# A hybrid decoder layer on one core: the first group of seven products in each feed-forward gets its weight sums and its accumulating transfer earlier

## The chip, the cores and the metric

The kernel runs on one core of one Trainium2 chip, as one program of one launch. The metric is the device time of an execution in microseconds (us). A profiled execution gives a trace of every instruction beside it.

## The reference, cut to what matters

One layer over 256 tokens and a model width of 1024, all in float32: a half-step feed-forward, a mixer (two kinds of attention, gated and merged), a second half-step feed-forward and a last norm.

```python
def swiglu(x, w_gate, w_up, w_down):
    return (jax.nn.silu(x @ w_gate) * (x @ w_up)) @ w_down
...
        h = h + FFN_RES * swiglu(rms_norm(h, ffn1_norm[l]), ffn1_w_gate[l], ffn1_w_up[l], ffn1_w_down[l])
        h = h + hybrid_mixer(rms_norm(h, mix_norm[l]), positions, w_in[l], b_gate[l],
                             w_branch_moba[l], w_branch_sb[l], w_out[l])
        h = h + FFN_RES * swiglu(rms_norm(h, ffn2_norm[l]), ffn2_w_gate[l], ffn2_w_up[l], ffn2_w_down[l])
    return rms_norm(h, final_norm)
```

The gate and up weights are 1024 x 2816, the down weights 2816 x 1024.

## The kernel before, in words

**Weights.** All weights stand in one stream of 376 tiles of 128 x 512, loaded two at a time: a chunk `raw{c}` holds tiles 2c and 2c+1 and is one transfer of 512 KB, issued by SP (`load`, line 188). Six chunks are in SBUF at a time (`RAW = 6`): the load of a chunk waits until the engines have read the chunk whose buffer it takes. A weight is used in two parts so that float32 precision is kept: ScalarE writes the rounded part `wh`, VectorE the rest `wl = raw - wh` (lines 228 and 229, or 232 and 233 with a gain), and TensorE makes three products from them (lines 370 to 372). The step that makes one pair `wh`, `wl` is `split`, and there is one for each *item*. Items are numbered in the order of use. Twelve pairs have buffers.

**Order of the work.** Nothing is scheduled by cost around the change: in both feed-forwards each engine executes its instructions in the order in which the program issues them (`manual_schedule`). Each `unit` issues three matmuls, lets one tick pass for the tasks that run beside (`weave`), and calls `W.pump()`, which issues at most one more `split`, if it is no more than `ahead` items ahead of the item in use. `ahead` is 7 for most of a feed-forward and 11 from its last gate-and-up block on.

**A feed-forward.** Eleven blocks of 8 items make the gate and up products, 256 hidden columns each (`gu_f`); the two halves of the tokens, t = 0 and 1, take turns with t = 1 two items behind. A block's result stands in a PSUM bank of a ring of three. `hidden` empties it: ScalarE's Silu (line 558), VectorE's product (line 559) into `sh_f`, VectorE's transpose in squares (line 567) into `hs_f`. For each pair of blocks, 16 small transfers `hm_f<-hs_f` of 32 KB (line 531) put the squares where the down product wants them, a few ticks apart, among the weight loads on SP's queue for the first four pairs of blocks and on GpSimd's for the last two. ScalarE and VectorE then split that too (`hth_f`, `htl_f`). The bank of block 9, t = 0 is taken again by block 10, t = 1.

**Sevens.** The down product works on groups of 2 x 128 hidden rows. Five of a feed-forward's groups use seven products in place of eight (a Strassen-like scheme), group 0 among them, which comes straight behind the gate and up blocks. Seven items j = 0 to 6 belong to such a group, with four tiles s to s+3 of the stream. Four of the seven weights are sums of tiles:

- tile s+1 gets tile s added by an accumulating transfer from HBM, issued by GpSimd (`summed`, line 200), nine items ahead of the group (`AHEAD_ADD = 9`);
- VectorE makes T2 = tile(s+1) + tile(s+3), T3 = T2 - tile(s), T4 = T2 + tile(s+2) (line 208), each in the `split` of the items j = 1, 2 and 3, just ahead of that item's `wh`. Items 4, 5 and 6 use T3, T2 and T4.

In the first feed-forward, items 80 to 87 are the last gate-and-up block, and items 88 to 94 are the seven of group 0, with chunks 44 and 45. The second feed-forward has the same order 259 items later, with chunks 166 and 167. The rows of its trace stand some 356.9 us behind the first one's.

Of the kernel before, what the change touches and what calls it, by code (L numbers as in the profile page):

```python
# [21 lines left out]
KD = D // P  # L22
FB = FF // 256
# [5 lines left out]
CH = 2  # L29
# [5 lines left out]
W_FFN2 = W_OUT + 2 * KD  # L35
# [30 lines left out]
AHEAD = 7  # L66
AHEAD_DOWN = 11
AHEAD_ADD = 9


INV_FREQ = [
# [30 lines left out]
class Weave:  # L102


    def __init__(self):
        self.now = 0
        self.tasks = []

    def add(self, gen, delay=0, long=False):
        self.tasks.append([self.now + delay, gen, long])  # L110
# [28 lines left out]
def _items():  # L139

    out, n = [], 0

    def plain(count):
        nonlocal n
        out.extend((n + i, None) for i in range(count))
        n += count

    for f in range(2):
        plain(FB * KD)
        for g in range(KF // 2):  # L150
            if g in SEVENS[f]:
                out.extend((n, j) for j in range(7))
                n += 4
            else:
                plain(4)
        if f == 0:
            plain(W_FFN2 - W_IN)
    assert n == N_TILES
    return out


class Weights:


    def __init__(self, nc, pool, early, sums, stream, gain, bufs, ahead):
        self.early, self.sums, self.items = early, sums, _items()
        self.nc, self.pool, self.stream, self.gain = nc, pool, stream, gain
        self.bufs, self.ahead = bufs, ahead
        self.loaded = self.ready = self.freed = self.at = 0
        self.raw, self.parts, self.behind = {}, {}, {}  # L170
        self.made, self.ahead_of = {}, {}
        self.depth = RAW
        for i, (s, j) in enumerate(self.items):
            if j == 0:
                self.ahead_of[i - AHEAD_ADD] = s

    def load(self, n, tiles=0):

# [18 lines left out]
    def summed(self, s):  # L197

        self.load(s // CH + 1)
        self.nc.gpsimd.dma_start(self.tile(s + 1), self.source(s), accum_op=ALU.add)  # L200

    def seventh(self, s, j):

        if 0 < j < 4:
            op, b, o = ((self.nc.vector.tensor_add, 3, "T2"), (self.nc.vector.tensor_sub, 0, "T3"),
                        (self.nc.vector.tensor_add, 2, "T4"))[j - 1]
            self.made[s, o] = self.sums(f"{o}_{s}")
            op(self.made[s, o], self.made[s, "T2"] if j > 1 else self.tile(s + 1), self.tile(s + b))
        raw = self.made.pop((s, f"T{(3, 2, 4)[j - 4]}")) if j > 3 else self.tile(s + (0, 2, 3, 1)[j])
        return raw, (s // CH, s // CH + 1) if j == 3 else ()  # L210

    def split(self):
        i = self.ready
        if i in self.ahead_of:
            self.summed(self.ahead_of.pop(i))
        s, j = self.items[i]
        used = (s // CH,) if s % CH == CH - 1 else ()
        if j is None:
            self.load(s // CH + 1)
            raw = self.tile(s)  # L220
        else:
            self.load(s // CH + (2 if j else 1))
            raw, used = self.seventh(s, j)
        hi = self.pool.tile([P, 512], F32R, name=f"wh{i}", tag="wh", bufs=self.bufs)
        lo = self.pool.tile([P, 512], F32R, name=f"wl{i}", tag="wl", bufs=self.bufs)
        g = self.gain(i)
        if g is None:
            self.nc.scalar.copy(hi, raw)  # L228
            self.nc.vector.tensor_sub(lo, raw, hi.bitcast(F32))  # L229
        else:  # L230
            for s in HALVES if i == 0 else (slice(0, 512),):
                self.nc.scalar.activation(hi[:, s], raw[:, s], AF.Copy, scale=g)  # L232
                self.nc.vector.scalar_tensor_tensor(lo[:, s], raw[:, s], g, hi[:, s].bitcast(F32),  # L233
                                                    op0=ALU.mult, op1=ALU.subtract)
        self.parts[i] = hi, lo
        self.ready += 1
        if i in self.behind:
            self.behind.pop(i)()
        for c in used:
            del self.raw[c]  # L240
            self.load(c + 1 + self.depth)
# [19 lines left out]
def hybrid_layer_kernel(ctx, tc, x, xt, pos, g_final, bgate, wstream, out):  # L261
# [164 lines left out]
    class Normed:  # L426
# [6 lines left out]
        def half(self, c, src=None):  # L433
            s = slice(c * 512, c * 512 + 512)
            src = h[self.t][:, s] if src is None else src
            tp = two_banks(f"tp_{self.nm}{self.t}{c}")[:, 0:512]
            for k in range(4):
                nc.tensor.transpose(tp[:, k * P:(k + 1) * P], src[:, k * P:(k + 1) * P], ident)
            split(self.parts[0][:, s], self.parts[1][:, s], tp)
            self.there.add(c)  # L440

        def moved(self, c):

            s = slice(c * 512, c * 512 + 512)
            if self.nm == "u" and self.t == 0:
                W.depth = RAW - 2
            q = big(f"{self.nm}q{self.t}{c}", F32)
            nc.vector.transpose(slots(q[:, 0:512], 4), plain(h[self.t][:, s]))
            W.ahead = AHEAD
            yield D_SQUARES  # L450
            queues = [nc.sync, nc.gpsimd]
            if self.nm == "u":
                queues = [nc.gpsimd, nc.sync, nc.gpsimd] if self.t else [nc.gpsimd, nc.scalar]
            elif self.t == 0:
                queues = [nc.gpsimd] + queues * 2
            yield from exchange(q[:, 512:1024], q[:, 0:512], 4, queues, 1)
            yield D_EIGHT
            split(plain(self.parts[0][:, s]), plain(self.parts[1][:, s]), slots(q[:, 512:1024], 4))
            self.there.add(c)

        @staticmethod
        def moved_both(c, norms):

            s = slice(c * 512, c * 512 + 512)
            squares, moved = [big(f"{norms[0].nm}{i}{c}", F32) for i in "sm"]
            for t in range(2):
                nc.vector.transpose(slots(squares, 8)[:, t:t + 7:2], plain(h[t][:, s]))
                yield None if t == 0 else D_SQUARES
            yield from exchange(moved, squares, 8, [nc.sync, nc.gpsimd], 1)
            yield D_BOTH  # L470
            for t in range(2):
                split(plain(norms[t].parts[0][:, s]), plain(norms[t].parts[1][:, s]), slots(moved, 8)[:, t:t + 7:2])
                norms[t].there.add(c)
                yield 1
# [815 lines left out]
```

## Time and profile before

| | |
|---|---|
| median of 3 runs | 546.92 us (546.83 to 547.07) |
| the profiled execution's own time | 547.5 us |
| its span, first to last instruction | 545.8 us |
| TensorE (PE) busy | 538.0 us, 99% of the span |
| VectorE (DVE) busy | 453.5 us, 83% |
| ScalarE (ACT) busy | 355.5 us, 65% |
| GpSimd (POOL) busy | 122.1 us, 22% |
| DMA, mean | 210 GB/s |

A row of a timeline has the start and the duration in us, the engine ("q" stands for its queue of DMA issues), the line of the kernel, what is written and read, the shapes and how many instructions the row merges; in brackets stands the idle time ahead of it with what ended it. Of a DMA, the row shows the issue; when it lands is read from the view of DMA issues, in us from the start of the issue. Buffer numbers are left out of the trace's names: `raw`, `wl` and `T` stand for all chunks, rests and sums.

### The profile page before, as it was taken

The page shows a single profiled execution, that of the slowest core. Times are in us where ns is not written, and L with a number is a line of the kernel's source. Part 1 is how long each engine was busy: PE and PEld are TensorE (multiplying, and loading weights), DVE is VectorE, ACT ScalarE, POOL GpSimd, SP SyncE. Part 2 cuts the span into 40 slices and gives each one's busy share as a digit, 9 for nine tenths or more (in the row PEclk, how much of TensorE's full clock was granted, in tenths as well). Part 3 has the DMA queues.
Part 4 walks back from the last instruction along what each step waited for, and adds up shares of the span by engine and source line. Part 5 has one row for each costly group of instructions (what it writes and reads, how often), then busy time and mean ns, then how long its engine had stood idle before and what let it go on. Part 6 is the DMA issues. An engine that isn't in the chain of part 4 may idle for free.

```text
span 545.8 us, 8032 instructions
## 1 busy us (share of the span) xinstructions
PE 538.0 (99%) x2460; PEld 444.4 (81%) x2460; DVE 453.5 (83%) x817; ACT 355.5 (65%) x620; POOL 122.1 (22%) x235
## 2 busy tenths in 40 slices
PE   9999999999999999999999999999999999999995
PEld 6888888888888888888888888888888888888884
DVE  5797799889999767889888888877667887899995
ACT  6776566667683777677875775466566566666843
POOL 2400000025503575022022200383000000265100
PEclk9999999999999999999999999999999999999998
DMA  8976765787866786455555354677657767787712
GB/s 280 406 263 220 239 209 184 231 254 225 257 225 191 274 261 217 154 155 191 170 161 175 125 188 153 195 244 233 215 180 223 221 201 236 233 227 237 238 49 77
DMA packets 44058, 114.84 MB, mean 210 GB/s; under 512 B 8512, under 2 KB 16240, under 8 KB 44016
## 3 DMA queue, kind: packets, MB, share of 16 engines
q1 hardware_dynamic: 37440, 106.68, 59.1%
q0 software_dynamic: 5904, 7.17, 6.0%
q10 hardware_dynamic: 672, 0.49, 0.3%
q8 instruction: 19, 0.31, 0.3%
q14 instruction: 23, 0.19, 0.1%
HBM read 104.87 MB, written 1.05 MB: 194 GB/s over the span
## 4 chain that ended last, share of the span: by engine, by line
PE 97%; DMA 1%; ACT 0%; SPq 0%; DVE 0%; issue 0%; ACTq 0%
PE gu_f L371 13%; PE gu_f L372 13%; PE gu_f L370 13%; PE in L370 7%; PE in L372 7%; PE in L371 7%; PE dn_f L371 5%; PE dn_f L372 5%; PE dn_f L370 5%; PE wo L372 1%; PE wo L370 1%; PE wo L371 1%; PE gu_f L383 1%; PE gu_f L384 1%; PE gu_f L386 1%; DMA raw<-in_wstream 1%
## 5 line engine op out<-in xcount | busy, mean ns | idle before, releaser
L233 DVE SCALAR_TENSOR_TENSOR wl<-raw,first,wh 128x512 fp32r<-128x512 f32 (+1 forms) x257 | 180.1, 742 | 24.0 <-ACT wh L232 23.5
L232 ACT ACTIVATE wh<-raw,first 128x512 fp32r<-128x512 f32 (+1 forms) x257 | 168.6, 714 | 26.1 <-PE gu_f L372 7.5
L229 DVE TENSOR_TENSOR wl<-raw,wh 128x512 fp32r<-128x512 f32 x120 | 78.7, 681 | 2.4 <-ACT wh L228 2.4
L228 ACT CAST wh<-raw 128x512 fp32r<-128x512 f32 x120 | 68.1, 618 | 18.2 <-PE bb L372 5.5
L371 PE MATMUL gu_f<-wl,zh 128*128 128x512 f32 x176 | 68.5, 389 | 0.0
L370 PE MATMUL gu_f<-wh,zh 128*128 128x512 f32 x176 | 68.5, 389 | 0.0
L372 PE MATMUL gu_f<-wh,zl 128*128 128x512 f32 x176 | 68.5, 389 | 0.0
L370 PE MATMUL in<-wh,uh 128*128 128x512 f32 x160 | 63.6, 397 | 0.0
L372 PE MATMUL in<-wh,ul 128*128 128x512 f32 x160 | 62.5, 391 | 0.0
L371 PE MATMUL in<-wl,uh 128*128 128x512 f32 x160 | 62.4, 390 | 0.0
L372 PE MATMUL gu_f<-wh,xl 128*128 128x512 f32 x144 | 56.0, 389 | 0.0
L370 PE MATMUL gu_f<-wh,xh 128*128 128x512 f32 x144 | 56.0, 389 | 0.0
L371 PE MATMUL gu_f<-wl,xh 128*128 128x512 f32 x144 | 56.0, 389 | 0.0
L200 POOL DMA_DIRECT2D raw<-in_wstream x10 | 9.4, 938 | 190.3 <-DVE cs_f L585 89.5
L370 PE MATMUL dn_f<-wh,hth_f 128*128 128x512 f32 x112 | 43.7, 390 | 0.0
L372 PE MATMUL dn_f<-wh,htl_f 128*128 128x512 f32 x112 | 43.6, 389 | 0.0
L371 PE MATMUL dn_f<-wl,hth_f 128*128 128x512 f32 x112 | 43.6, 389 | 0.0
L531 POOL DMA_DIRECT2D hm_f<-hs_f x64 | 34.3, 681 | 22.7 <-DMA raw<-in_wstream 9.3
L370 PEld LDWEIGHTS gu_f<-wh,zh 128*128 128x128 f32 x176 | 33.0, 188 | 6.9
L372 PEld LDWEIGHTS gu_f<-wh,zl 128*128 128x128 f32 x176 | 33.0, 188 | 6.8
L371 PEld LDWEIGHTS gu_f<-wl,zh 128*128 128x128 f32 x176 | 33.0, 188 | 6.8
L372 PEld LDWEIGHTS in<-wh,ul 128*128 128x128 f32 x160 | 30.0, 188 | 6.5
(320 smaller groups left out, 991.8 us busy)
## 6 DMA issues: line engine op xcount, KB each, us to landing
raw<-in_wstream SPq DMA_DIRECT2D x185, 512.0 KB, 4.5
hm_f<-hs_f SPq DMA_DIRECT2D x128, 32.0 KB, 4.1
raw<-in_wstream POOLq DMA_DIRECT2D x10, 256.0 KB, 4.6
raw<-in_wstream SPq DMA_DIRECT2D x5, 256.0 KB, 5.4
h<-in_x SPq DMA_DIRECT2D x2, 512.0 KB, 8.3
hm_f<-hs_f POOLq DMA_DIRECT2D x32, 32.0 KB, 3.9
bg<-in_bgate POOLq DMA_DIRECT2D x4, 256.0 KB, 5.1
xin<-in_xt SPq DMA_DIRECT2D x2, 256.0 KB, 6.6
```

Source lines behind the costliest of these rows:

```text
L200: self.nc.gpsimd.dma_start(self.tile(s + 1), self.source(s), accum_op=ALU.add)
L228: self.nc.scalar.copy(hi, raw)
L229: self.nc.vector.tensor_sub(lo, raw, hi.bitcast(F32))
L232: self.nc.scalar.activation(hi[:, s], raw[:, s], AF.Copy, scale=g)
L233: self.nc.vector.scalar_tensor_tensor(lo[:, s], raw[:, s], g, hi[:, s].bitcast(F32), op0=ALU.mult, op1=ALU.subtract)
L370: nc.tensor.matmul(o, ah, wh, start=first, stop=False)
L371: nc.tensor.matmul(o, ah, wl, start=False, stop=False)
L372: nc.tensor.matmul(o, al, wh, start=False, stop=last)
L383: nc.tensor.matmul(o, ah, wh, start=first, stop=False)
L384: nc.tensor.matmul(o, al, wh, start=False, stop=False)
L386: nc.tensor.matmul(o, ah, wl, start=False, stop=last)
L531: queues[m % len(queues)].dma_start(moved[j * w:j * w + w, i * n * w:(i + 1) * n * w], squares[i * w:i * w + w, j * n * w:(j + 1) * n * w])
```

## The change

For the group of seven that follows a plain item right at the end of the gate and up blocks, in each feed-forward, the accumulating transfer is issued 14 items ahead instead of 9, and T2, T3 and T4 are made 6, 5 and 4 items ahead of the group instead of in its items 1, 2 and 3. The other four groups of seven stay as they were. The adding itself moves into a method `add`, which first asks for the chunks that it reads, and does nothing when the sum is there already.

```diff
+AHEAD_FIRST = 14, (6, 5, 4)
...
             if j == 0:
-                self.ahead_of[i - AHEAD_ADD] = s
+                steps = [(AHEAD_ADD, self.summed)]
+                if self.items[i - 1][1] is None and i - W_FFN2 in (FB * KD, FB * KD - W_FFN2):
+                    lead, leads = AHEAD_FIRST
+                    steps = [(lead, self.summed)] + [(n, lambda s, j=j: self.add(s, j + 1)) for j, n in enumerate(leads)]
+                for lead, step in steps:
+                    self.ahead_of.setdefault(i - lead, []).append((step, s))
...
+    def add(self, s, j):
+
+        op, b, o = ((self.nc.vector.tensor_add, 3, "T2"), (self.nc.vector.tensor_sub, 0, "T3"),
+                    (self.nc.vector.tensor_add, 2, "T4"))[j - 1]
+        if (s, o) not in self.made:
+            self.load(s // CH + 2)
             self.made[s, o] = self.sums(f"{o}_{s}")
             op(self.made[s, o], self.made[s, "T2"] if j > 1 else self.tile(s + 1), self.tile(s + b))
...
-        if i in self.ahead_of:
-            self.summed(self.ahead_of.pop(i))
+        for step, s in self.ahead_of.pop(i, ()):
+            step(s)
```

The following rows are VectorE's in the first feed-forward before the change, from the rest of item 85 (`wl85`) to T4 of the group that begins with item 88. `sh_f19_0` is the product tile of block 9, t = 0.

```order
L233 SCALAR_TENSOR_TENSOR wl85_1329<-raw42_1164,first_73,wh85_1328 128x512
L559 SCALAR_TENSOR_TENSOR sh_f19_0_1338<-gu_f19_0_1234,r_x0_129,sh_f19_0_1338 128x256
L567 STREAM_TRANSPOSE hs_f18_1221<-sh_f19_0_1338 128x2x4x32
L559 SCALAR_TENSOR_TENSOR sh_f19_1_1353<-gu_f19_1_1269,r_x1_130,sh_f19_1_1353 128x256
L567 STREAM_TRANSPOSE hs_f18_1221<-sh_f19_1_1353 128x2x4x32
L233 SCALAR_TENSOR_TENSOR wl86_1358<-raw43_1188,first_73,wh86_1357 128x512
L233 SCALAR_TENSOR_TENSOR wl87_1366<-raw43_1188,first_73,wh87_1365 128x512
L229 TENSOR_TENSOR wl88_1375<-raw44_1212,wh88_1374 128x512
L208 TENSOR_TENSOR T2_88_1384<-raw44_1212,raw45_1260 128x512
L229 TENSOR_TENSOR wl89_1387<-raw45_1260,wh89_1386 128x512
L208 TENSOR_TENSOR T3_88_1394<-T2_88_1384,raw44_1212 128x512
L229 TENSOR_TENSOR wl90_1397<-raw45_1260,wh90_1396 128x512
```

And these are VectorE's rows after the change, from the rest of item 81 on.

```order
L245 SCALAR_TENSOR_TENSOR wl81_1281<-raw40_1105,first_73,wh81_1280 128x512
L215 TENSOR_TENSOR T2_88_1293<-raw44_1175,raw45_1260 128x512
L245 SCALAR_TENSOR_TENSOR wl82_1296<-raw41_1142,first_73,wh82_1295 128x512
L215 TENSOR_TENSOR T3_88_1306<-T2_88_1293,raw44_1175 128x512
L245 SCALAR_TENSOR_TENSOR wl83_1309<-raw41_1142,first_73,wh83_1308 128x512
L215 TENSOR_TENSOR T4_88_1321<-T2_88_1293,raw45_1260 128x512
L245 SCALAR_TENSOR_TENSOR wl84_1324<-raw42_1164,first_73,wh84_1323 128x512
L245 SCALAR_TENSOR_TENSOR wl85_1335<-raw42_1164,first_73,wh85_1334 128x512
L571 SCALAR_TENSOR_TENSOR sh_f19_0_1344<-gu_f19_0_1235,r_x0_129,sh_f19_0_1344 128x256
L579 STREAM_TRANSPOSE hs_f18_1222<-sh_f19_0_1344 128x2x4x32
```

The three sums moved from between the rests of items 88 to 91 to between those of items 81 to 84, ahead of the products of block 9.

The second place is SP's queue of transfers in the same stretch, before the change, from the load of chunk 42 to that of chunk 46. `hm_f13` belongs to the fourth pair of blocks, 6 and 7.

```order
L188 DMA raw42_1164<-in_wstream 128x1024
L531 DMA hm_f13_1155<-hs_f16_971 32x256 x2
L188 DMA raw43_1188<-in_wstream 128x1024
L531 DMA hm_f13_1155<-hs_f16_971 32x256 x2
L188 DMA raw44_1212<-in_wstream 128x1024
L531 DMA hm_f13_1155<-hs_f16_971 32x256 x3
L188 DMA raw45_1260<-in_wstream 128x1024
L531 DMA hm_f13_1155<-hs_f16_971 32x256
L188 DMA raw46_1284<-in_wstream 128x1024
```

After the change the same stretch reads as follows.

```order
L194 DMA raw42_1164<-in_wstream 128x1024
L543 DMA hm_f13_1155<-hs_f16_971 32x256
L194 DMA raw43_1173<-in_wstream 128x1024
L194 DMA raw44_1175<-in_wstream 128x1024
L543 DMA hm_f13_1155<-hs_f16_971 32x256 x6
L194 DMA raw45_1260<-in_wstream 128x1024
L543 DMA hm_f13_1155<-hs_f16_971 32x256
L194 DMA raw46_1284<-in_wstream 128x1024
```

Since the accumulating transfer, issued 14 items ahead, asks for chunk 44, the loads of chunks 43 and 44 moved up past small transfers, chunk 43 past one and chunk 44 past three; chunk 45 keeps its place. The orders of ScalarE, TensorE and GpSimd do not change.

More of the change, by code (lines that the diff above doesn't have):

```diff
@@ L200, in summed @@
         self.nc.gpsimd.dma_start(self.tile(s + 1), self.source(s), accum_op=ALU.add)
+    def add(self, s, j):
[3 more added lines that the diff above has]
+            self.load(s // CH + 2)
+            self.made[s, o] = self.sums(f"{o}_{s}")
+            op(self.made[s, o], self.made[s, "T2"] if j > 1 else self.tile(s + 1), self.tile(s + b))
     def seventh(self, s, j):
         if 0 < j < 4:
[L205 to L208, printed above, removed]
+            self.add(s, j)
         raw = self.made.pop((s, f"T{(3, 2, 4)[j - 4]}")) if j > 3 else self.tile(s + (0, 2, 3, 1)[j])
```

## The prediction

> **What bounds the kernel now.** First come the page's totals and the chain that ended last.
>
> ```profile
> span 545.8 us, 8032 instructions
> PE 538.0 (99%) x2460; PEld 444.4 (81%) x2460; DVE 453.5 (83%) x817; ACT 355.5 (65%) x620; POOL 122.1 (22%) x235
> ...
> PE 97%; DMA 1%; ACT 0%; SPq 0%; DVE 0%; issue 0%; ACTq 0%
> ```
>
> TensorE is on that chain for 97% of the span. Busy time alone would not prove that it never starves, since its ends are modelled, so two more views: what PE waited for in the whole execution, and its busy time in a stretch around group 0 of each feed-forward.
>
> ```profile
> PE warm L361 <- DVE zeros L340: 1.1, 1, 1.1
> PE gu_f L383 <- ACT wh L232: 0.3, 1, 0.3
> ...
> 90.00:160.00 70.00, 70.00 (x311) 57.96 (x310) 65.97 (x122) 49.47 (x86) 20.67 (x37) 1.00 0.77 237
> ...
> 450.00:520.00 70.00, 70.00 (x311) 57.98 (x310) 64.38 (x113) 48.57 (x86) 20.49 (x37) 1.00 0.76 234
> ```
>
> Both waits belong to the start. Around the change TensorE starts 311 matmuls in 70 us, one every 0.226 us, at a granted clock of 1.00, and is never idle. So nothing in these stretches waits for the sums that the change moves: it has no stall to remove. It can only leave the time as it is, or make TensorE wait where it does not wait now. The question is whether the earlier place of the sums costs more than the cover that VectorE has there.
>
> **VectorE's stretch.** This is VectorE's timeline in the first feed-forward. The row with x2 at 99.69 is the rests of items 76 and 77; the row with x5 at 109.06 is items 81 to 85; the two L559 rows are block 9's products; the T row is T2.
>
> ```profile
> 99.69 1.41 DVE L233 SCALAR_TENSOR_TENSOR wl<-raw,first,wh 128x512 fp32r<-128x512 f32 x2
> ...
> 109.06 3.39 DVE L233 SCALAR_TENSOR_TENSOR wl<-raw,first,wh 128x512 fp32r<-128x512 f32 x5
> 113.49 0.48 DVE L559 SCALAR_TENSOR_TENSOR sh_f<-gu_f,r_x,sh_f 128x256 f32<-128x256 f32 x1 [1.04 <-ACT sh_f L558]
> 114.01 0.45 DVE L567 STREAM_TRANSPOSE hs_f<-sh_f 128x256 f32<-128x256 f32 x1
> 115.59 0.48 DVE L559 SCALAR_TENSOR_TENSOR sh_f<-gu_f,r_x,sh_f 128x256 f32<-128x256 f32 x1 [1.14 <-ACT sh_f L558]
> ...
> 117.77 0.68 DVE L229 TENSOR_TENSOR wl<-raw,wh 128x512 fp32r<-128x512 f32 x1
> 118.38 0.68 DVE L208 TENSOR_TENSOR T<-raw,raw 128x512 f32<-128x512 f32 x1
> 118.98 0.68 DVE L229 TENSOR_TENSOR wl<-raw,wh 128x512 fp32r<-128x512 f32 x1
> ```
>
> A rest with a gain takes a place of 0.66 us on the queue ((3.39 - 0.74) / 4, the last one's own 0.74 left out), a sum 0.60 (118.98 - 118.38). The new order wants T2 where the rest of item 82 stands, at 109.06 + 0.66 = 109.7. The two idle times of 1.04 and 1.14 us would swallow the 1.8 us of three sums.
>
> **When T2 can start.** It reads chunk 44 with its accumulated half, and chunk 45. Their transfers, as SP and GpSimd issue them in the two feed-forwards (chunk 44 at 102.00 and 457.87, its accumulation at 107.81 and 463.76, chunk 45 at 107.91 and 464.77):
>
> ```profile
> 102.00 0.53 SPq L188 DMA_DIRECT2D raw<-in_wstream  x1
> ...
> 107.91 0.33 SPq L188 DMA_DIRECT2D raw<-in_wstream  x1
> ...
> 107.81 1.11 POOL L200 DMA_DIRECT2D raw<-in_wstream  x1 [78.89 <-DVE cs_f L586]
> ...
> 457.87 0.53 SPq L188 DMA_DIRECT2D raw<-in_wstream  x1
> ...
> 464.77 0.33 SPq L188 DMA_DIRECT2D raw<-in_wstream  x1
> ...
> 463.76 0.94 POOL L200 DMA_DIRECT2D raw<-in_wstream  x1 [89.50 <-DVE cs_f L585]
> ```
>
> The view of DMA issues, asked for each of them alone, gives the time to landing: chunk 44, the accumulation and chunk 45 of the first feed-forward, then the same of the second.
>
> ```profile
> raw<-in_wstream SPq DMA_DIRECT2D x1, 512.0 KB, 5.1
> ...
> raw<-in_wstream POOLq DMA_DIRECT2D x1, 256.0 KB, 6.3
> ...
> raw<-in_wstream SPq DMA_DIRECT2D x1, 512.0 KB, 3.6
> ...
> raw<-in_wstream SPq DMA_DIRECT2D x1, 512.0 KB, 5.0
> ...
> raw<-in_wstream POOLq DMA_DIRECT2D x1, 256.0 KB, 3.9
> ...
> raw<-in_wstream SPq DMA_DIRECT2D x1, 512.0 KB, 4.5
> ```
>
> So the accumulation goes out 0.7 us (107.81 - 107.1) and 0.9 us (463.76 - 462.9) after chunk 44 has landed. The VectorE instructions named in its brackets are only the last that ended before. Issuing it 14 items ahead buys little: chunk 44 takes the buffer of chunk 38, whose last reader is the rest of item 77, done at 99.69 + 1.41 = 101.1. Its load thus moves from 102.00 to 101.1, 0.9 earlier. I take the accumulation to move by as much, to 106.9. Chunk 45 waits for the rest of item 79, which does not move: it stays at 107.91.
>
> In the changed first feed-forward the accumulation is then 1.0 us ahead of chunk 45, as it already is in the second (464.77 - 463.76). I therefore use that pair: the accumulation lands at 106.9 + 3.9 = 110.8, chunk 45 at 107.9 + 4.5 = **112.4**, and T2 starts there, 2.7 us after its place came up. In the second feed-forward the accumulation goes out at 462.9, 1.9 us ahead of chunk 45, and lands at 466.8. Chunk 45's transfer then meets less of it, and takes between 3.6 and 4.5; with the middle, T2 starts at 464.77 + 4.0 = **468.8**.
>
> **What is queued behind T2.** On VectorE: four rests, two sums, then block 9's products, which empty a PSUM bank. TensorE wants that bank for block 10, t = 1, three units of three matmuls after block 10 began at 114.82. The rows are block 10's first matmul, then the first into that bank in both feed-forwards, then the one place where TensorE does start on a semaphore, 0.05 us after its releaser's end (7.79 + 0.73).
>
> ```profile
> 114.82 0.39 PE L370 MATMUL gu_f<-wh,xh 128*128 128x512 f32 x1
> ...
> 116.86 0.39 PE L370 MATMUL gu_f<-wh,xh 128*128 128x512 f32 x1
> ...
> 473.74 0.39 PE L370 MATMUL gu_f<-wh,zh 128*128 128x512 f32 x1
> ...
> 7.79 0.73 ACT wh L232
> ...
> 8.57 0.50 PE gu_f L383
> ```
>
> From T2's start to the free bank it takes 3 x 0.60 + 4 x 0.66 + 0.48 + 0.05 = 4.97 us. T2 must therefore start by 116.86 - 4.97 = 111.89 and by 473.74 - 4.97 = 468.77. Before, the product ended at 113.97, 2.9 us early.
>
> **The sum.** First feed-forward: 112.4 - 111.9 = 0.5 us of stall. Second: 468.8 against 468.8, nothing. TensorE has no idle time to win it back, so the profiled execution's 547.5 would become 548.0; its 547.5 is 0.6 above the median of 546.92, which becomes **547.4**.
>
> Bounds, from the nearest rows: with the shortest times (3.9 for the accumulation, 3.6 for chunk 45) T2 starts at 111.5 and nothing stalls. With the accumulation unmoved and at its longest, 107.81 + 6.3 = 114.1, the stall is 2.2; in the second 462.9 + 6.3 = 469.2 costs 0.4. A gain has no place to come from, except that no execution of the new order has been seen.
>
> By the fit in the Trainium skill (DMA: Bandwidth & Descriptors, Anatomy of one DMA) a transfer from GpSimd's queue has about 2.0 us of fixed cost and moves 436 KB in a us, which makes 2.6 us, an estimate, for these 256 KB. By it the accumulation would land at 109.5, before T2's place comes up; the trace has 3.9 and 6.3, so the measured times stand.
>
> **What else moves.** These rows are of SP's timeline, VectorE's, and the page's part on DMA issues: the small transfers around chunk 43's load, chunk 48's load and the last three small transfers, then the next uses, which are the split of the moved squares and the next group's T2.
>
> ```profile
> 98.85 1.24 SPq L531 DMA_DIRECT2D hm_f<-hs_f  x2
> ...
> 113.25 0.53 SPq L188 DMA_DIRECT2D raw<-in_wstream  x1
> 113.82 2.67 SPq L531 DMA_DIRECT2D hm_f<-hs_f  x3
> ...
> 126.45 1.22 DVE L402 TENSOR_TENSOR htl_f<-hm_f,hth_f 128x1024 fp32r<-128x1024 f32 x1
> ...
> 130.56 0.69 DVE L208 TENSOR_TENSOR T<-raw,raw 128x512 f32<-128x512 f32 x1
> ...
> hm_f<-hs_f SPq DMA_DIRECT2D x128, 32.0 KB, 4.1
> ```
>
> The second small transfer of the first row now stands behind both loads, at 101.7 instead of about 99.6: some 2 us late, for squares that are split 25 us later. Chunk 48's load waits for the rest of item 85, which ends at 112.4 + 3 x 0.60 + 3 x 0.66 + 0.74 = 116.9 (3.7 later than before). It lands 5.1 later, at 122.0; its accumulation, 0.7 and then at worst 6.3 later, lands at 129.0, before 130.56. The last squares go out behind it, by 119.5 (2.67 for the three), and need 4.1, to 123.6, before 126.45. Both hold with more than a us to spare, so I cost them at nothing; without that cover each us of lateness would be a us of TensorE. By the end of the group VectorE has its 1.8 us of sums behind it, and is about as late as TensorE itself (0.4 to 0.5), so the stall does not return further on.
>
> **The rivals.**
>
> *The accumulation comes late (slower).* Chunk 45's packets get ahead of it, as in the first feed-forward before, and it takes 6.3. T2 starts at 106.9 + 6.3 = 113.2, or 114.1 if its issue does not move. The stalls are 1.3 to 2.2 and 0.4: 548.6 to 549.5. It decides from a T2 later than 113.0. For it: the 6.3 stands in this very place. Against: there the accumulation was issued only 0.1 ahead of chunk 45, now 1.0. Chance 0.26.
>
> *Nothing stalls (no change).* Everything lands by 111.9 and 468.8, and the time stays at 546.9. For it: chunk 45's own 3.6 there; its margin is only 0.5 us away. Against: that 3.6 was measured with the accumulation behind it. The estimate of 2.6 us by the Trainium skill (DMA: Bandwidth & Descriptors) would lead here as well. Chance 0.28.
>
> *Faster.* Some wait of TensorE on a rest of group 0, hidden in modelled ends, goes. Each start 0.226 us after the last speaks against it; at most the sums' 1.8 us in each feed-forward, 543.3. Chance 0.04.
>
> **How the numbers follow.** The forecast, one short stall in the first feed-forward (up to 1.09 us in all), has 0.42: 547.4. A measurement of this kernel can tell about 0.2%, 1.09 us, from no change; so the forecast and the second rival both count as the same, 0.70, slower has 0.26 and faster 0.04. The range begins 0.2 below the median, for its spread and the case without a stall, and reaches to 549.0 into the late accumulation, whose upper half (1 in 10) it leaves out.
>
> **What would show it.** Right: on VectorE a first T row at about 112.4 with an idle time of 2.7 us ahead of it that a DMA ended, and about 468.8 in the second; the product of block 9 near 116.8; one new row in PE's waits, on the product L571, of 0.5 us; the accumulation landing within 4 us. Wrong: no idle time ahead of T2 (the chunks land sooner than I think), a stall of over 1 us, or a PE wait for anything but that bank: then the chain through the bank is not the one that decides.

## The result, and the profile after

The changed kernel takes 549.94 us, the median of six runs (549.1 to 552.15), beside 547.0 for the kernel before (546.51 to 548.12). The ratio is 1.0057, with a 95% interval of 1.0036 to 1.0078: slower by 0.57%, where the forecast was 547.4 us, which is no change within the noise. (A ratio here and below is not that of the two medians, which would be 1.0054, so they need not match to the last digit.) The profiled execution took 550.97 us, 3.5 more than the one before. It is 1.0 above its median, as the one before was 0.5 above its own.

In the changed kernel the product is line 571, a sum 215, an accumulation 206, a raw load 194, and the gate-and-up matmuls 382 to 384. The page's totals and the chain that ended last:

```profile
span 549.3 us, 8027 instructions
PE 538.5 (98%) x2460; PEld 443.6 (81%) x2460; DVE 454.0 (83%) x817; ACT 356.0 (65%) x620; POOL 122.6 (22%) x235
...
PE 81%; DVE 9%; DMA 6%; issue 2%; SPq 1%; ACT 0%; POOLq 0%; ACTq 0%; DVEq 0%
```

The work is the same on every engine to within 0.5 us, and to within 0.8 for the weight loads (PEld). What is new is that the chain leaves TensorE for 19% of the span, where it left it for 3% before. That is not lost time: from each stall the chain runs back through VectorE and the transfers, beside which TensorE was at work. What PE waited for, and the two stretches around the change:

```profile
PE gu_f L382 <- DVE sh_f L571: 3.3, 2, 2.9
```

```profile
90.00:160.00 70.00, 67.15 (x295) 55.00 (x294) 62.79 (x111) 46.95 (x82) 20.67 (x37) 1.00 0.75 223
450.00:520.00 70.00, 69.60 (x307) 57.34 (x306) 63.89 (x112) 46.89 (x83) 20.51 (x37) 1.00 0.78 234
```

TensorE now idles 2.85 us in the first feed-forward and 0.40 in the second, both times for block 9's product on VectorE. It is one wait in two places, and no other wait was added. TensorE's timeline shows the two places: the last matmul ahead of each gap and the one behind it.

```profile
116.11 0.40 PE L384 MATMUL gu_f<-wh,xl 128*128 128x512 f32 x1
119.36 0.50 PE L382 MATMUL gu_f<-wh,xh 128*128 128x512 f32 x1 [2.85 <-DVE sh_f L571]
...
476.29 0.39 PE L384 MATMUL gu_f<-wh,zl 128*128 128x512 f32 x1
477.08 0.50 PE L382 MATMUL gu_f<-wh,zh 128*128 128x512 f32 x1 [0.40 <-DVE sh_f L571]
```

At one start every 0.23 us the gaps cost 3.25 - 0.23 = **3.02 us** and 0.79 - 0.23 = **0.56 us**. Together that is 3.6, against 3.5 between the spans, but the two are not the same sum. The execution after is 0.77 us ahead of the one before from early on: a load at 60.36 us before stands at 59.59 after, far ahead of the change. Followed matmul by matmul, TensorE falls back by 3.39 us around the first stall (the starts next to the gap are some 0.1 late each), by 0.15 between the feed-forwards and by 0.69 around the second stall; with the 0.77 taken off, that makes the 3.5. So nearly all of the loss is these two stalls. In this stretch 0.77 is added below where a time is put "on the clock of before".

VectorE's timeline in the first feed-forward, from the rest of item 81 to block 9's product (the row with x2 is the rests of items 84 and 85):

```profile
108.29 0.74 DVE L245 SCALAR_TENSOR_TENSOR wl<-raw,first,wh 128x512 fp32r<-128x512 f32 x1
114.36 0.69 DVE L215 TENSOR_TENSOR T<-raw,raw 128x512 f32<-128x512 f32 x1 [5.33 <-DMA raw<-in_wstream]
...
117.50 1.41 DVE L245 SCALAR_TENSOR_TENSOR wl<-raw,first,wh 128x512 fp32r<-128x512 f32 x2
118.83 0.48 DVE L571 SCALAR_TENSOR_TENSOR sh_f<-gu_f,r_x,sh_f 128x256 f32<-128x256 f32 x1
```

VectorE stands still for 5.33 us ahead of T2, where the prediction had 2.7. The product then starts 4.47 us behind T2, and TensorE 5.00 behind it. T2's start is 115.1 on the clock of before; the limit had been 111.9. What it waited for stands in the chain that ended last, here between 100 and 120 us, with the start and length of each piece:

```profile
100.33 6.63 DMA raw<-in_wstream
106.96 0.03 POOLq L206
...
107.69 6.65 DMA raw<-in_wstream
...
114.36 0.04 DVE T L215
...
118.91 0.41 DVE sh_f L571
119.31 0.04 issue
119.36 0.50 PE gu_f L382
```

The chain reads: chunk 44's load, 6.6 us; then its accumulation, issued at 107.69, another 6.65; then T2; then the product; then the matmul. SP's and GpSimd's queues show how the accumulation stands to chunk 45's load, which is the row at 107.14:

```profile
100.33 0.33 SPq L194 DMA_DIRECT2D raw<-in_wstream  x1
100.72 3.69 SPq L543 DMA_DIRECT2D hm_f<-hs_f  x6
107.14 0.33 SPq L194 DMA_DIRECT2D raw<-in_wstream  x1
...
107.69 1.11 POOL L206 DMA_DIRECT2D raw<-in_wstream  x1 [78.20 <-DMA hm_f<-hs_f]
```

The accumulation goes out 0.55 us *behind* chunk 45's load, not 1.0 ahead of it. Chunk 45 itself was quick: the view of DMA issues gives it 3.3 us, so it had landed at 110.4, four microseconds before T2.

```profile
raw<-in_wstream SPq DMA_DIRECT2D x1, 512.0 KB, 3.3
```

In the second feed-forward the accumulation went out at 466.61, 0.94 ahead of chunk 45's load (467.55), and took 4.0; chunk 45 took 4.4 and landed last, at 471.96. VectorE's timeline there (the bracket names a small transfer, but T2 does not read it, and it landed at 472.2, behind T2's start; of the transfers that T2 reads, chunk 45's came last):

```profile
472.08 0.69 DVE L215 TENSOR_TENSOR T<-raw,raw 128x512 f32<-128x512 f32 x1 [2.64 <-DMA hm_f<-hs_f]
...
476.55 0.47 DVE L571 SCALAR_TENSOR_TENSOR sh_f<-gu_f,r_z,sh_f 128x256 f32<-128x256 f32 x1
```

### The profile page after: what moved, and what is told of

The parts are those of the page before. It is cut to its first block, busy times and chain, and to the rows that moved or that the text cites. A ratio compares the mean times of both kernels' runs of the same rounds, so it can differ in the third digit from the quotient of the medians.

```text
span 549.3 us, 8027 instructions
## 1 busy us (share of the span) xinstructions
PE 538.5 (98%) x2460; PEld 443.6 (81%) x2460; DVE 454.0 (83%) x817; ACT 356.0 (65%) x620; POOL 122.6 (22%) x235
## 4 chain that ended last, share of the span: by engine, by line
PE 81%; DVE 9%; DMA 6%; issue 2%; SPq 1%; ACT 0%; POOLq 0%; ACTq 0%; DVEq 0%
PE gu_f L382 8%; PE gu_f L384 8%; PE gu_f L383 8%; PE in L382 7%; PE in L384 7%; PE in L383 7%; DVE wl L245 6%; PE dn_f L384 5%; PE dn_f L383 5%; PE dn_f L382 5%; DMA hm_f<-hs_f 3%; DMA raw<-in_wstream 2%; PE wo L382 1%; PE wo L384 1%; PE wo L383 1%
```

## The experiments

**What had to be told apart.** My reading of the trace is that T2, moved ahead of block 9's products, waits for its operands, and that everything behind it on VectorE waits with it, up to the product that frees TensorE's bank. Against it stood two rivals. One is the transfer half of the change: loads that pass small transfers on SP's queue, and an accumulation that meets another load. The other is plain work: 1.8 us of sums ahead of the product would make it late even if nothing waited. A second question was why the accumulation took 6.65 us where 3.9 was taken.

**The transfer half alone.** The accumulation goes 14 items ahead, the sums stay where they were.

```diff
-                    steps = [(lead, self.summed)] + [(n, lambda s, j=j: self.add(s, j + 1)) for j, n in enumerate(leads)]
+                    steps = [(lead, self.summed)]
```

> The accumulating transfer stays 14 items ahead, the three sums go back into the group's items 1 to 3. Theory (T2 waits for its transfers at its new place, and block 9's products, which free TensorE's bank, stand behind it on VectorE): without the early sums nothing is late, so the time of before, 547.0 within 0.2%, and no wait of TensorE on the product. Rival (the two weight loads that moved up past the small transfers on SP cost the time): about 549.9, as after the change.

Measured: 547.06 us, ratio 0.9998 (0.999 to 1.0007). TensorE's stretches, in the same windows as before:

```profile
90.00:160.00 70.00, 70.00 (x311) 57.96 (x310) 65.96 (x117) 49.77 (x88) 20.66 (x37) 1.00 0.77 236
450.00:520.00 70.00, 70.00 (x311) 57.96 (x310) 64.75 (x112) 48.67 (x87) 20.49 (x37) 1.00 0.77 235
```

No start is lost. The passing on SP's queue and the earlier accumulation cost nothing, and bring nothing. The first rival falls.

**The sums alone.** The accumulation keeps its old lead of nine.

```diff
-AHEAD_FIRST = 14, (6, 5, 4)
+AHEAD_FIRST = 9, (6, 5, 4)
```

> The sums are made 6, 5 and 4 items ahead, the transfer goes back to 9 items ahead. Theory: T2 waits for the accumulation as it landed before the change, at about 114.1 on the first feed-forward's clock, so the stall is 2.2 there and about 0.5 in the second: 549.5 to 550, as slow as the whole change, because the 14 items bring the transfer nothing. Rival (the earlier transfer shortens T2's wait): clearly slower than the whole change, 551 or more.

Measured: 550.44 us, ratio 1.0053 (1.0036 to 1.007): the whole loss, and 0.4 above what I expected. The execution that was profiled is the fastest of these runs (548.32), so its trace shows the smaller end. VectorE's first sum in it, and what PE waited for:

```profile
112.02 0.69 DVE L215 TENSOR_TENSOR T<-raw,raw 128x512 f32<-128x512 f32 x1 [3.17 <-DMA raw<-in_wstream]
```

```profile
PE gu_f L382 <- DVE sh_f L571: 1.2, 2, 1.0
```

It is the same pair of stalls, 1.1 and 0.4 us, behind a T2 that waits 3.2 instead of 5.3. Here the accumulation took 5.1. So the early sums make the loss, and its size goes with the landing. That the slower runs, which have no trace, waited longer at the same place is argued, not shown; their granted clocks, 0.996 to 0.999, are those of the runs of before, which speaks against the clock as the reason.

**The same work without the wait.** The three sums of the two first groups read tiles that landed long before, at the same places of the queue. Those three weights, and what is computed with them, are then not the reference's.

```diff
+FIRSTS = 88, 332
...
-            op(self.made[s, o], self.made[s, "T2"] if j > 1 else self.tile(s + 1), self.tile(s + b))
+            a, b = (s + 1, s + b) if s not in FIRSTS else (s - 6, (s - 5, s - 5, s - 4)[j - 1])
+            op(self.made[s, o], self.made[s, "T2"] if j > 1 else self.tile(a), self.tile(b))
```

> The whole change, but for the two first groups the sums read tiles of chunks that have long landed (so these three weights are not the reference's): same instructions at the same places, no wait for chunk 44's accumulation nor for chunk 45. Theory: 547.0 within 0.2%, with T2 at its place straight behind the rest of item 81 and the product of block 9 near 114.2. Rival (the 1.8 us of sums ahead of block 9's products are themselves too much for VectorE there): about 549, with TensorE still waiting for the product.

Measured: 547.11 us, ratio 1.0 (0.9989 to 1.001). VectorE's first sum and block 9's product:

```profile
109.20 0.69 DVE L217 TENSOR_TENSOR T<-raw 128x512 f32<-128x512 f32 x1
...
113.66 0.48 DVE L573 SCALAR_TENSOR_TENSOR sh_f<-gu_f,r_x,sh_f 128x256 f32<-128x256 f32 x1
```

T2 has no idle time ahead of it. The product stands 4.46 us behind T2, as in the changed kernel, but 5.4 us earlier on the clock of before (this execution is 0.53 ahead of it), and TensorE loses no start. So the place and the work are free, and the wait is the cost. The second rival falls too. The accumulation still took 6.84 us in this run, with nobody waiting for it.

**No accumulating transfer.** For the two first groups VectorE adds the two tiles itself, just ahead of T2.

```diff
+        if s in FIRSTS:
+            return
         self.nc.gpsimd.dma_start(self.tile(s + 1), self.source(s), accum_op=ALU.add)
...
+            if s in FIRSTS and j == 1:
+                self.nc.vector.tensor_add(self.tile(s + 1), self.tile(s + 1), self.tile(s))
             op(self.made[s, o], self.made[s, "T2"] if j > 1 else self.tile(s + 1), self.tile(s + b))
```

> For the two first groups VectorE adds tile s to tile s+1 just ahead of T2 (one more sum of 0.6 us) and the accumulating transfer is left out; the rest is the whole change. Theory (in the first feed-forward the accumulation lands last, 3 to 4 us behind chunk 45): T2 starts when chunk 45 has landed, about 111.2 to 111.6, which is in time for the bank (111.9), so 547.0 to 547.3. Rival (chunk 45 is as late as the accumulation): 549 or more.

Measured: 547.02 us, ratio 0.9994 (0.9985 to 1.0003). VectorE's first sum:

```profile
110.78 0.69 DVE L220 TENSOR_TENSOR T<-raw,raw 128x512 f32<-128x512 f32 x1 [0.90 <-DMA raw<-in_wstream]
```

With 0.6 us more of VectorE's work the loss is gone, since T2 then waits only for chunk 45: 0.90 us, inside the cover. In the first feed-forward the accumulation is what came last, and not chunk 45.

**Less ahead of the product.** Two kernels leave the accumulation at 14 and put the sums later: at leads 4, 3, 2 two of them, and at 3, 2, 1 one of them, stand ahead of the product.

```diff
-AHEAD_FIRST = 14, (6, 5, 4)
+AHEAD_FIRST = 14, (4, 3, 2)
```

> The whole change with the sums 4, 3 and 2 items ahead instead of 6, 5 and 4: T2 stands behind the rest of item 83, and between T2 and the product of block 9 lie one sum, two rests less (2 x 0.60 + 2 x 0.66 = 2.52 us to the product's start instead of 4.44). Theory (T2 waits for a landing, and what lies between it and the bank is added): each stall shrinks by 1.9, from 3.0 to about 1.1 in the first feed-forward and from 0.6 to nothing in the second: 547.5 to 548.3. Rival (any early sum delays the bank by its whole wait, whatever lies between): 549 to 550.

Measured at 4, 3, 2: 548.06 us, ratio 1.0008 (0.9999 to 1.0016). VectorE's T2 and the product:

```profile
114.31 0.69 DVE L215 TENSOR_TENSOR T<-raw,raw 128x512 f32<-128x512 f32 x1 [3.79 <-DMA raw<-in_wstream]
...
116.85 0.47 DVE L571 SCALAR_TENSOR_TENSOR sh_f<-gu_f,r_x,sh_f 128x256 f32<-128x256 f32 x1
```

T2 starts as late as in the changed kernel, but the product is only 2.54 us behind it, so TensorE stalls 1.1 us in the first feed-forward and not at all in the second. That is as expected, but it stands on the trace: by the times alone this kernel cannot be told from before.

> The sums 3, 2 and 1 items ahead: only T2 and the rest of item 85 (0.60 + 0.66 = 1.26 us) lie ahead of the product of block 9, 3.2 us less than in the change. Theory: no stall unless T2 starts later than 115.1 on the clock of before; 547.0 within 0.2%, or up to 547.4 where an execution's landing is that late. Rival: 548 or more.

Measured at 3, 2, 1 (the same line of the code): 547.17 us, ratio 1.0003 (0.9995 to 1.0012), with no stall. T2 still waited:

```profile
112.58 0.69 DVE L215 TENSOR_TENSOR T<-raw,raw 128x512 f32<-128x512 f32 x1 [1.41 <-DMA raw<-in_wstream]
```

The product follows 1.27 us later, within the cover. A wait of VectorE costs by what is queued between it and the product; its length alone does not decide.

**Was the accumulation slow as GpSimd's first transfer?** Its row in the timeline has 78 us of idle time ahead of it. In this kernel GpSimd issues a small transfer at the start, and the rest is as changed.

```diff
-    nc.sync.dma_start(posi, pos)
+    nc.gpsimd.dma_start(posi, pos)
```

> The whole change, with one tiny load of the start (the positions, 128 x 2) issued by GpSimd instead of SP, so that the first group's accumulation is no longer the first transfer that GpSimd issues. It has taken 5.1 to 6.8 us in the first feed-forward and 3.9 in the second in each trace so far. Theory on this (the first transfer by GpSimd is slow to start): it takes about 4 to 4.5 us now, T2 starts 2 us sooner, and the time is 547.3 to 548.2. Rival (chunk 45's load beside it makes it slow): still 5 to 7 us, and 549 to 550.

Measured: 550.15 us, ratio 1.0057 (1.0037 to 1.0077). The accumulation took 6.94 us. It was not slow for being the first, and this explanation falls. The profiled execution took 554.02, 3.1 more than that of the changed kernel, with the same stall. TensorE's timeline behind it, then the granted clock (the 1.00 or 0.50 behind the last bracket) in the windows next to it:

```profile
119.70 0.80 PE L382 MATMUL gu_f<-wh,xh 128*128 128x512 f32 x1 [2.85 <-DVE sh_f L571]
120.30 0.63 PE L383 MATMUL gu_f<-wl,xh 128*128 128x512 f32 x1
120.72 0.63 PE L384 MATMUL gu_f<-wh,xl 128*128 128x512 f32 x1
```

```profile
112.00:116.00 4.00, 4.00 (x19) 3.10 (x17) 1.29 (x3) 1.81 (x4) 0.00 (x0) 1.00 0.47 158
120.00:125.00 5.00, 5.00 (x13) 3.85 (x13) 4.96 (x10) 1.24 (x2) 1.72 (x4) 0.50 0.83 258
126.00:131.00 5.00, 5.00 (x24) 4.10 (x23) 2.80 (x5) 3.09 (x6) 1.20 (x3) 1.00 0.93 270
```

For some 5 us behind the stall the matmuls start every 0.43 us at a granted clock of 0.50. The 13 in the window would have taken 13 x 0.23 = 3.0 us, so about 2 us are lost there and some 2.7 over the whole stretch (119.70 to about 125.4). The same stall in the changed kernel's own profile was not followed by this:

```profile
119.40:125.00 5.60, 5.60 (x25) 4.64 (x26) 5.57 (x11) 2.38 (x4) 1.23 (x3) 1.00 0.80 231
```

**Chunk 44 ahead of chunk 43.** If the accumulation is slow because it shares the transfer engines with chunk 45's load, it should be quick with a longer lead. Here chunks 43 and 44 (and 165 and 166) are loaded in the other order.

```diff
+SWAPPED = {43: 44, 44: 43, 165: 166, 166: 165}
...
             c, j = divmod(self.loaded, CH)
+            c = SWAPPED.get(c, c)
```

> The whole change, but the load of chunk 44 goes ahead of that of chunk 43 in the first feed-forward (166 ahead of 165 in the second), so that it is issued behind the rest of item 75 instead of 77 and the accumulation well over 1 us ahead of chunk 45's load. Theory (an accumulation issued together with chunk 45's load shares the transfer engines with it and takes 5 to 7 us, one issued 1 us ahead takes 4): it takes about 4 in the first feed-forward too and lands before chunk 45, T2 starts with chunk 45's landing, and the time is 547.0 to 547.7. Rival (an accumulation is slow at this place whatever is beside it): it takes 5 to 7 us again; T2 still starts sooner, so the trace decides, by its duration.

Measured: 548.41 us, ratio 1.0019 (1.0009 to 1.0028), slower than expected. The accumulation in GpSimd's timeline, then it and chunk 45's load (issued at 107.24) in the view of DMA issues, then VectorE's T2:

```profile
105.44 1.11 POOL L208 DMA_DIRECT2D raw<-in_wstream  x1 [75.56 <-DMA hm_f<-hs_f]
```

```profile
raw<-in_wstream POOLq DMA_DIRECT2D x1, 256.0 KB, 4.1
...
raw<-in_wstream SPq DMA_DIRECT2D x1, 512.0 KB, 5.1
```

```profile
112.45 0.69 DVE L217 TENSOR_TENSOR T<-raw,raw 128x512 f32<-128x512 f32 x1 [3.31 <-DMA raw<-in_wstream]
```

With a lead of 1.8 us the accumulation took 4.1 instead of 6.65 and landed at 109.5, as sharing would have it, although its first 1.4 us lay beside the end of chunk 43's load. But chunk 45's load now took 5.1 instead of 3.3 and landed at 112.4, and T2 waited for that: stalls of 1.25 and 0.2 us. My expectation let the accumulation speed up and left chunk 45 as it was. What the accumulation gained, the load lost in large part.

**One item further ahead.** As a test of the price by the queue: one more rest between T2 and the product.

```diff
-AHEAD_FIRST = 14, (6, 5, 4)
+AHEAD_FIRST = 14, (7, 6, 5)
```

> The whole change with the sums 7, 6 and 5 items ahead: one more rest (0.66 us) between T2 and the product of block 9. Theory: each stall grows by 0.66, to about 3.7 and 1.2, so 1.3 more than the change: 551 to 552 if TensorE's clock holds, and 2 to 3 more in executions in which the idle time makes it drop, as the trace of the run with the positions loaded by GpSimd showed (matmuls 0.43 us apart for 5 us behind a stall of 3.0). Rival (the stall is set by T2's landing alone): as the change, 550.

Measured: 552.03 us, ratio 1.0085 (1.0065 to 1.0104). VectorE's T2 and the product, then what PE waited for, in an execution of 550.52 us, near the fast end of its runs:

```profile
112.65 0.69 DVE L215 TENSOR_TENSOR T<-raw,raw 128x512 f32<-128x512 f32 x1 [3.88 <-DMA raw<-in_wstream]
...
117.78 0.48 DVE L571 SCALAR_TENSOR_TENSOR sh_f<-gu_f,r_x,sh_f 128x256 f32<-128x256 f32 x1
```

```profile
PE gu_f L382 <- DVE sh_f L571: 2.7, 2, 1.7
```

The product is 5.13 us behind T2 instead of 4.47, by the one rest of 0.66. From start to start the stalls are 1.8 and 1.24 us. The second is the 0.56 of the changed kernel and 0.66 more, as expected; the first is smaller than there because the operands landed early in this execution (the accumulation took 5.2). The times alone do not show the step, since the interval of this ratio overlaps that of the changed kernel.

Taken together, the traces bear the price out closely. T2 must start by 111.89 on the clock of before, or by 1.92 later (leads 4, 3, 2) or 0.66 earlier (leads 7, 6, 5) where less or more is queued behind it. T2's start less that limit is 3.24 us in the changed kernel, 1.09 with the sums alone, 1.12 at leads 4, 3, 2, 1.23 with the chunks swapped and 1.79 at leads 7, 6, 5. TensorE's first matmul into the bank is late by 3.26, 1.11, 1.13, 1.25 and 1.82. (Each execution is put on the clock of before by its own shift: 0.77, 0.96, 0.62, 0.67 and 0.37.)

No version beats the kernel before: TensorE already started a matmul every 0.226 us there. The transfer half alone, VectorE's own addition, and leads 3, 2, 1 equal it.

## Why the prediction was wrong

- **The bound was right.** "It can only leave the time as it is, or make TensorE wait where it does not wait now." There was no stall to remove, and every variant is equal or slower.
- **The mechanism was right.** T2 waits for a landing, block 9's product waits behind T2, and TensorE waits for its bank: the new row in PE's waits is the one named, on line 571. From T2's start to TensorE's the prediction had 4.97 us, and the trace has 5.00.
- **The step that failed** is "I take the accumulation to move by as much, to 106.9", and with it "I therefore use that pair". Chunk 44's load did go out 0.9 earlier (100.33 + 0.77 = 101.1, against 102.00). It did not land earlier: it took 6.6 us where it had taken 5.1, and landed at 107.7 on the clock of before, against 107.1. So the accumulation went out at 108.5 on that clock: 1.6 later than I took, and even 0.65 later than before. That put it behind chunk 45's load, and the pair to use was the first feed-forward's own (6.3), not the second's (3.9); it took 6.65. The two errors, 1.6 and 2.75, put its landing 4.3 us later than predicted, at 115.1 instead of 110.8. Chunk 45, which I had as the last to land, at 112.4, was there at 111.2.
- **The second feed-forward** failed at the same step, by a smaller size. Chunk 44's load went out 0.9 earlier there too and landed no earlier (465.96, or 463.2 on the clock of before with the shift of 2.78 that holds there, against 462.9), so the accumulation was only 0.94 ahead of chunk 45 and not 1.9. The limit for T2 there is 476.52 - 5.00 = 471.52, with 476.52 as the start that the row at 476.29 would have been followed by. Chunk 45's load went out 3.97 us ahead of that limit, as predicted (468.77 - 464.77 = 4.0), but took 4.4 and not 4.0. With 0.1 from landing to start, that is the 0.56 us. Whether the shorter lead made the difference is not shown: in these traces leads of 0.9 to 1.7 go with 4.2 to 5.4 us for this load, a lead of 2.4 with 4.1, and no accumulation with 3.5.
- **The bounds** stopped too early. The latest T2 was put at 114.1, with the accumulation unmoved and 6.3 long. It was 115.1, as the accumulation can also go out later than before, and the longest row of one trace is not the longest that there is.
- **The edits costed at nothing** cost nothing: the transfer half alone has a ratio of 0.9998, and in the changed kernel PE waits for no squares and for no later group. (The "3.7 later than before" there is against the load's issue at 113.25; the rest itself had ended at 112.45.)
- **The rival with 0.26** is what happened. It named the mechanism and the point from which it decides (a T2 later than 113.0). What spoke against it, "now 1.0" of lead, rested on the step that failed. Its price of 548.6 to 549.5 ends 0.4 below the median, as its stalls end at 2.2 and 0.4 where the trace has 3.0 and 0.56.

What stays open is why chunk 44's load takes longer when it is issued earlier. Over the runs with the transfer half, issued 0.9 us earlier, it landed between 3.0 and 2.1 us ahead of the end of the rest of item 81, against 2.7 before. So the earlier issue moved the landing by anything from 0.4 earlier to 0.6 later. Chunk 43's load, right ahead of it, grew too, from 4.9 to 6.0 us in the changed kernel's trace. That fits two loads that share a full set of transfer engines, but no run took the other transfers away.

## What to carry to other kernels

Work moved earlier on an in-order engine makes everything behind it wait for its operands. Its price is the landing, plus the work queued from there to the next buffer that another engine needs, less the time at which that engine needs it; the queued work is counted from the order of instructions, and the length of the wait alone does not give the price. An earlier issue need not be an earlier landing: here a load issued 0.9 us earlier landed anywhere from 0.4 earlier to 0.6 later. Take the landing unmoved, and ask which transfers change places behind it. Where the critical engine has no gap, look for what a change can delay before asking what it can gain.

## What the runs showed of the hardware

**Transfers that share.** The accumulation's time goes with its lead over the 512 KB load of chunk 45. These are the first feed-forwards, with the lead counted from the accumulation's issue to chunk 45's:

| kernel | lead, us | accumulation, us |
|---|---|---|
| chunks swapped | 1.80 | 4.09 |
| leads 3, 2, 1 | 0.42 | 5.69 |
| transfer half alone | 0.28 | 5.94 |
| before | 0.10 | 6.26 |
| leads 7, 6, 5 | 0.08 | 5.17 |
| sums alone | 0.02 | 5.06 |
| leads 4, 3, 2 | -0.06 | 6.94 |
| small transfer first | -0.26 | 6.94 |
| sums that do not wait | -0.35 | 6.84 |
| changed kernel | -0.55 | 6.65 |

Issued behind the load it takes 6.65 to 6.94, up to 0.4 ahead of it 5.1 to 6.3, and 1.8 ahead of it 4.1. Near a lead of zero it can fall either way. In the second feed-forwards of the same ten traces the leads are 0.9 to 2.4, and the accumulation took 3.75 to 4.4. The Trainium skill (DMA: Bandwidth & Descriptors, Issuing engines are not separate DMA queues) says that transfers started by different engines run on the same 16 DMA engines and interleave. The swapped chunks agree: the accumulation of GpSimd gained 2.5 us and the load of SP lost 1.8.

**A stall that costs twice.** Of two executions with the same stall, 2.85 us of idle TensorE at the same place, one went on at a granted clock of 1.00 and the other at 0.50 for some 5 us, which cost about 2.7 us more. The Trainium skill (TensorE: Matmul & The Clock Gate, What's actually happening) has the clock fall to half after at least one idle window of about 3.4 us, in windows that run freely. Here an idle time of 2.85 us by the profile (3.25 from start to start) was enough, so the measurement decides: the figure is no safe limit. The fall even stands at 118.7, inside the stall and only 1.9 us behind the end of the last matmul.

The traces also show what differs between the two executions. Every stretch of one granted clock that lies wholly within a trace is a whole multiple of 3.41 us long: 6.83, 112.6 and 423.3 us in the run with the small transfer first, 535.9 or 539.3 in the other ten. On this grid the same stall is cut at different places. The rows are two neighbouring pieces of the grid in the run with the small transfer first, in the changed kernel and at leads 7, 6, 5; the second number behind the window is TensorE's busy time, and the granted clock is the third from the end.

```profile
115.29:118.70 3.41, 1.56 (x6) 0.67 (x4) 3.41 (x7) 3.14 (x6) 0.00 (x0) 1.00 0.14 20
118.70:122.11 3.41, 2.41 (x6) 1.93 (x7) 3.34 (x7) 0.62 (x1) 0.54 (x1) 0.50 0.86 286
...
114.62:118.03 3.41, 1.89 (x8) 0.94 (x6) 3.41 (x6) 3.41 (x7) 0.00 (x0) 1.00 0.02 4
118.03:121.44 3.41, 2.08 (x9) 1.75 (x10) 3.34 (x8) 0.68 (x2) 0.51 (x1) 1.00 0.86 254
...
116.12:119.53 3.41, 1.75 (x8) 1.14 (x7) 3.34 (x8) 2.52 (x6) 0.00 (x0) 1.00 0.75 256
119.54:122.95 3.41, 3.41 (x16) 2.79 (x16) 3.41 (x7) 1.70 (x3) 0.54 (x1) 1.00 0.91 278
```

A piece with 1.56 us of work was followed by half the clock, and pieces with 1.75 and 1.89 were not; at the ends of the executions, pieces with up to 1.5 were followed by 0.50 as well. So these traces fit a clock that falls when TensorE is busy for less than about half of such a piece, and then the place of a stall on the grid counts beside its length. The busy times are modelled, and no run moved a stall along the grid on purpose, so this is a reading of eleven traces and not a tested rule.

The runs of the changed kernel spread over 3 us (549.1 to 552.15), where before spreads over 1.6. A fall of the clock does not look like the reason: their mean granted clocks are 0.996 and 0.997, as in the runs of before (0.996 to 0.999). Lower means stand only beside the two slowest runs with the small transfer first (0.991 and 0.993) and the two slowest at leads 7, 6, 5 (0.994 and 0.995). Landings that differ from execution to execution would fit the spread, but that is argued, not shown.
